# A filler sweep that projects the merge gates before the branch gates

## The chip, the core and the metric

The kernel runs on one core of a Trainium2 chip. Its engines work from queues of their own, each in a fixed order: TensorE (PE), VectorE (DVE), ScalarE (ACT), GpSimd (POOL), and SyncE (SP), which here only issues DMAs. ACT and POOL issue DMAs too. The metric is the time of one execution on the device in microseconds, lower is better.

## What is computed

One step of a decoder layer for 2048 prompt tokens and 32 sample tokens (8 groups of 4), in fp32:

```python
h = _rmsnorm(x, g_pre) @ w_in
qa, ka, va, za, ub, zb, qc, zc, gt = jnp.split(h, SPLITS, axis=-1)
# A: dilated window attention -> oa; B: conv, LayerNorm, swish -> ob; C: attention into a memory -> oc
gates = jax.nn.sigmoid(gt).reshape(Bx, S, 3, D_MODEL)
mix = (gates[..., 0, :] * ((oa * jax.nn.silu(za)) @ w_pa)
       + gates[..., 1, :] * ((ob * jax.nn.silu(zb)) @ w_pb)
       + gates[..., 2, :] * ((oc * jax.nn.silu(zc)) @ w_pc))
y = x + _rmsnorm(mix @ w_out, g_post)
```

The case concerns the columns of `w_in` for za (768), zb (768), zc (512) and the merge gates gt (3072). They are not needed until the last phase.

## The kernel before

Activations are kept transposed, with 128 channels on the partitions and tokens along the free axis. Every fp32 operand is split into a high and a low part, and a product is three matmuls (lines 166, 167, 168 in `gemm`: high by high, high by low, low by high). A block is 128 output columns of `w_in`. Its weights are one DMA of 512 KB (line 150), split on POOL (lines 55 and 56).

Phase A1 normalizes the tokens and computes q, k, v, the convolution input and qc, with the convolution's taps on DVE (line 322). The LayerNorm of the convolution then runs in steps of 256 tokens (`conv_norm`, lines 663 to 686): a load, a sum on DVE (665), a matmul with ones on PE (667), a subtraction (668), squares on ACT (671), a sum (673), a matmul (675), variance and reciprocal root on DVE and ACT (677, 63 to 68), scaling (679), per-channel scale on POOL (681), tanh on ACT (684), and a product on DVE (685). Beside it the memory's keys and values are projected (917 to 947), and the prompt's and sample's attention into the memory follow. After it come the sample attention (791 to 869) and the prompt attention, six head pairs with two heads each (571 to 652). At the end of a pair the three dilation patterns are combined: statistics go through DRAM (427 to 441), coefficients come back as broadcast DMAs `cb<-d_cf` (448), and DVE and POOL multiply and add (451 to 453). Phase C multiplies branch outputs by their gates z (1139), splits them (1197 on ACT, 1198 on DVE), projects and merges (1150 to 1155), and applies the output projection (1178 to 1180).

The sweep is a generator that runs beside all of this from the LayerNorm to the end of the attention. It computes the 40 blocks of za, zb, zc and gt. The tokens come in three thirds of 768, 768 and 544, of whose normalized values one is held at a time; at the start of the second and third POOL loads the next one (1083). In each third the sweep takes the blocks in the order of a list, and each block in chunks of 256 tokens (288 at the very end): 3, 3 and 2 chunks, so 120, 120 and 80, 320 in all. A chunk is 24 matmuls into one of two PSUM buffers `gg`, followed by the part of `chunk` that reads it into one of two staging tiles `st`:

```python
elif kind == "gt":
    nc.scalar.activation(st[:, :n], p[:, :n], AF.Tanh, scale=0.5)                      # line 243, ACT
else:
    nc.scalar.activation(st[:, :n], p[:, :n], AF.Tanh, scale=0.5)                      # line 245, ACT
    nc.vector.scalar_tensor_tensor(st[:, :n], st[:, :n], 1.0, p[:, :n],
                                   op0=ALU.add, op1=ALU.mult)                          # line 246, DVE
if dst is not None:
    q.dma_start(dst[j][:, s:s + n], st[:, :n])                                         # line 248, ACT's queue
```

So a gate chunk (gt) is finished by ACT, while a z chunk (za, zb, zc) needs ACT and then DVE, reads PSUM in both, and its store on ACT's queue waits for DVE. 192 chunks are of the first kind and 128 of the second.

No loop in the program interleaves the sweep with the rest. Its instructions are written last (one call, `self.fill(1000)`), and the builder orders each engine's instructions by a timeline that it estimates, in which what is written earlier goes first and the sweep fills what is left. The order is fixed when the program is built. The first block's weights are loaded ahead, at the end of phase A1 (`self.early`).

Of the kernel before, what the change touches and what calls it, by code (L numbers as in the profile page):

```python
# [26 lines left out]
EARLY = 1  # L27
# [7 lines left out]
CQ, CK, CV, CZA, CUB, CZB, CQC, CZC, CGT = 0, 768, 1536, 2304, 3072, 4608, 5376, 5888, 6400  # L35


class K:
# [134 lines left out]
    def phase_a1(self, wp, blocks=None):  # L173
        tc, nc, I, O = self.tc, self.nc, self.I, self.O
        with tc.tile_pool(name="x12", side="right", bufs=1) as xpool, \
                tc.tile_pool(name="stg", side="right", bufs=3) as stg, \
                tc.tile_pool(name="sm1", side="right", bufs=2) as small, \
                tc.tile_pool(name="wr", side="right", bufs=2) as self.wr, \
                tc.tile_pool(name="psg", side="right", bufs=4, space=PSUM, reuse_waits="tile") as psg, \
                tc.tile_pool(name="pst", side="right", bufs=3, space=PSUM, reuse_waits="tile") as pst:  # L180
            for th in (1, 2):
                n = THIRDS[th][1]
                self.X[th] = tuple([xpool.tile([128, n], R32, name=f"x{th}{c}{k}") for k in range(8)]
                                   for c in "hl")
            with tc.tile_pool(name="xst", side="right", bufs=7) as xst:
                st = self.stage_x(xst, small, pst)
                next(st)
                self.consts(self.cpool, xst, pst)
                ws = [self.load_w(wp, self.win(CQ), 8, rp=self.wr)]
                for _ in st:  # L190
                    pass
            with tc.tile_pool(name="brw", side="right", bufs=1) as bp:
                self.taps(self.cpool, bp, pst)
                self.bias_rows(self.cpool, bp, pst)

            out = [(th, c, k) for th in (1, 2) for c in range(2) for k in range(8)]

            with tc.tile_pool(name="cnv", side="right", bufs=1, reuse_waits="tile") as cnv:
                ws.append(self.load_w(wp, self.win(CQ + 128), 8, rp=self.wr))
                for cs, js in [(c, j) for c in (CHUNKS[:1], CHUNKS[1:2], CHUNKS[2:3], CHUNKS[3:4], CHUNKS[4:]) for j in range(2)]:  # L200
                    for s, n in cs:
                        self.chunk("q", js, s, n, ws[js], stg, psg, "g", pst)
                order = []
                rest = [("k", j) for j in range(6)] + [("v", j) for j in range(6)] + \
                       [("q", j) for j in range(2, 6)] + [("qc", j) for j in range(4)]
                for j in range(6):
                    order += [("u", j)] + rest[:3]
                    rest = rest[3:]
                order += rest
                for kind, j in order:  # L210
                    if blocks is not None and (kind, j) not in blocks:
                        continue
                    if kind == "u":
                        gs = self.blk_u(j, wp, stg, cnv, psg, pst)
                        with self.later(LAG):
                            self.conv(j, cnv, pst, *gs)
                    else:
                        self.blk_x(kind, j, wp, stg, psg, pst)
                    for th, c, k in out[:2]:
                        nc.sync.dma_start(self.d_x[th][c][k], self.X[th][c][k].bitcast(F32))  # L220
                    del out[:2]
                assert not out
                self.early = {("za", j): self.load_w(wp, self.win(CZA + 128 * j), 8, rp=self.wr) for j in range(EARLY)}
    def blk_x(self, kind, j, wp, stg, psg, pst):
        w = self.load_w(wp, self.win(self.BASE[kind] + j * 128), 8, rp=self.wr)
        for s, n in CHUNKS:
            self.chunk(kind, j, s, n, w, stg, psg, "g", pst)
# [973 lines left out]
    def build(self):  # L1201
        tc, nc = self.tc, self.nc
        with tc.tile_pool(name="dr", bufs=1, space=DRAM) as dp, tc.tile_pool(name="cst", bufs=1) as cp:
            self.scratch(dp)
            self.cpool = cp
            with tc.tile_pool(name="x0", bufs=1) as x0, tc.tile_pool(name="w1", bufs=2) as wp:
                self.X = [tuple([x0.tile([128, 768], R32, name=f"x0{c}{k}") for k in range(8)] for c in "hl"), None, None]
                self.phase_a1(wp)
                with tc.tile_pool(name="gst", bufs=2, reuse_waits="tile") as gp, tc.tile_pool(name="pgg", bufs=2, space=PSUM, reuse_waits="tile") as pgg:
                    blocks = [(k, j) for k, n in (("za", 6), ("zb", 6), ("zc", 4), ("gt", 24)) for j in range(n)]  # L1210
                    self.filler, self.credit = self.sweep(blocks, x0, wp, gp, pgg), 0
                    with tc.tile_pool(name="sbk", side="right", bufs=1, reuse_waits="tile") as sk:
                        self.memory()
                        self.sample_bias(sk)
                        self.sample_attention()
                    self.attention(list(range(HA)))
                    self.fill(1000)
            self.phase_c()
# [89 lines left out]
```

## Time and profile before

| | us |
|---|---|
| median of 3 runs (3150.18 to 3156.21) | 3155.59 |
| the profiled execution, its own time | 3154.4 |
| its span from first to last instruction | 3152.6 |
| PE busy | 3000.2 |
| DVE busy | 2014.8 |
| ACT busy | 1124.2 |
| POOL busy | 1350.4 |
| first and last matmul of the sweep | 868.7 and 2549.7 |

Times in the views count from the first instruction. "Busy" of PE is the time in which any matmul is under way; idle time of an engine is put down to what ended it, written with an arrow (`PE gg L166 <- DVE st L246`: a matmul into `gg`, line 166, waited for line 246 on DVE). Names are the program's tiles with their numbers left out, written out<-in. A wait is one inferred from semaphores; where an instruction waits for several, the last one is named. The granted clock is the share of full speed that TensorE was given.

### The profile page before, as it was taken

What the parts mean: (1) busy time and instruction counts of PE and PEld (TensorE: products, weight loads), DVE (VectorE), ACT (ScalarE), POOL (GpSimd) and SP (SyncE); (2) the same over time, 40 slices, a digit from 0 to 9 for tenths busy, and PEclk for the clock granted to TensorE, in tenths of its full rate; (3) what the DMA queues carried; (4) which work ended last, traced back from release to release, by engine and by line L of the source; (5) the groups of instructions that cost most, each with busy time, mean ns of one, the idle gap of its engine ahead of it and who ended that gap; (6) DMA issues with size and microseconds to landing.
All of it is one profiled execution on the core that took longest, in us unless ns stands there. A gap on an engine that the chain in (4) does not pass through costs nothing.

```text
span 3152.6 us, 55374 instructions
## 1 busy us (share of the span) xinstructions
PE 3000.2 (95%) x20705; PEld 2839.9 (90%) x20705; DVE 2014.8 (64%) x3734; ACT 1124.2 (36%) x2835; POOL 1350.4 (43%) x1048
## 2 busy tenths in 40 slices
PE   7999999999987999999999999989899979999998
PEld 6899999999987999998999999989898967787897
DVE  5297797796677926465546766666656457556563
ACT  5010010010132433243437575656565523222221
POOL 0121221142356537444256565667676433233240
PEclk9899999999999999999999999999999989999999
DMA  7232222211265454477454656576555487657561
GB/s 250 85 103 80 80 60 61 63 62 50 81 182 167 135 153 144 147 219 239 151 139 116 161 123 163 128 185 150 156 143 152 109 279 227 223 168 227 161 197 53
DMA packets 532218, 454.66 MB, mean 144 GB/s; under 512 B 118191, under 2 KB 458581, under 8 KB 531137
## 3 DMA queue, kind: packets, MB, share of 16 engines
q1 hardware_dynamic: 357502, 335.36, 36.2%
q10 hardware_dynamic: 169840, 105.02, 11.7%
q0 software_dynamic: 4608, 10.75, 1.2%
q8 instruction: 164, 2.69, 0.4%
q14 instruction: 104, 0.85, 0.1%
HBM read 332.96 MB, written 118.04 MB: 143 GB/s over the span
## 4 chain that ended last, share of the span: by engine, by line
PE 70%; DMA 12%; DVE 7%; issue 4%; POOL 3%; ACT 2%; SPq 1%; ACTq 0%; DVEq 0%; POOLq 0%
PE g L166 8%; PE g L167 8%; PE g L168 8%; PE gg L166 6%; PE gg L168 6%; PE gg L167 6%; PE pg L168 3%; PE pg L166 3%; PE pg L167 3%; PE pt L571 2%; DMA cb<-d_cf 2%; PE y L1180 2%; PE y L1179 2%; PE y L1178 2%; PE o L598 1%
## 5 line engine op out<-in xcount | busy, mean ns | idle before, releaser
L166 PE MATMUL gg<-x0h,whi 128*128 128x256 f32 (+1 forms) x2560 | 747.9, 292 | 25.9 <-DVE st L246 12.2
L168 PE MATMUL gg<-x0h,wlo 128*128 128x256 f32 (+1 forms) x2560 | 741.8, 290 | 0.1
L167 PE MATMUL gg<-x0l,whi 128*128 128x256 f32 (+1 forms) x2560 | 741.1, 290 | 0.0
L55 POOL TENSOR_SCALAR whi<-wraw 128x1024 fp32r<-128x1024 f32 x162 | 242.7, 1500 | 928.5 <-PE g L167 524.1
L166 PEld LDWEIGHTS gg<-x0h,whi 128*128 128x128 f32 x2560 | 493.2, 193 | 35.0 <-DVE st L246 13.7
L167 PEld LDWEIGHTS gg<-x0l,whi 128*128 128x128 f32 x2560 | 493.5, 193 | 2.2 <-issue 0.5
L168 PEld LDWEIGHTS gg<-x0h,wlo 128*128 128x128 f32 x2560 | 493.2, 193 | 2.2 <-POOL wlo L56 0.3
L322 DVE SCALAR_TENSOR_TENSOR acc<-G,cw,acc 128x1536 f32<-128x1536 f32 (+15 forms) x354 | 480.8, 1408 | 0.3
L56 POOL TENSOR_TENSOR wlo<-wraw,whi 128x1024 fp32r<-128x1024 f32 x162 | 417.0, 2575 | 9.4 <-PE gg L168 0.2
L155 POOL TENSOR_TENSOR clo<-craw,chi 128x768 fp32r<-128x768 f32 (+1 forms) x96 | 174.1, 1815 | 346.0 <-ACT chi L154 329.8
L627 ACT ACTIVATE P<-T,stm 128x128 f32<-128x128 f32 (+1 forms) x576 | 260.8, 455 | 141.0 <-DVE stm L625 94.8
L239 ACT ACTIVATE st<-g 128x384 f32<-128x384 f32 (+1 forms) x132 | 60.2, 461 | 570.7 <-PE g L168 550.7
L166 PE MATMUL pg<-ac,chi 128*128 128x512 f32 (+1 forms) x640 | 229.4, 359 | 16.6 <-ACT chi L154 8.7
L625 DVE CUSTOM_DVE_ANT_0 T<-s,bias 128x128 f32<-128x128 f32 (+1 forms) x576 | 191.5, 357 | 80.8 <-PE s L617 47.0
L167 PE MATMUL pg<-ac,chi 128*128 128x512 f32 (+1 forms) x640 | 228.8, 358 | 6.3 <-DVE ac L1198 6.3
L168 PE MATMUL pg<-ac,clo 128*128 128x512 f32 (+1 forms) x640 | 227.6, 357 | 3.6 <-POOL clo L155 3.6
L576 DVE TENSOR_TENSOR pl<-pt,ph 128x512 fp32r<-128x512 f32 x240 | 155.6, 652 | 52.4 <-ACT ph L575 48.9
L168 PE MATMUL g<-x0h,wlo 128*128 128x384 f32 x544 | 184.3, 339 | 2.9 <-POOL wlo L56 2.9
L166 PE MATMUL g<-x0h,whi 128*128 128x384 f32 x544 | 183.6, 338 | 2.6 <-ACT st L239 2.3
L167 PE MATMUL g<-x1l,whi 128*128 128x384 f32 x544 | 186.0, 342 | 0.0
L167 PE MATMUL g<-x0l,whi 128*128 128x384 f32 x544 | 185.8, 342 | 0.0
L168 PE MATMUL g<-x1h,wlo 128*128 128x384 f32 x544 | 185.8, 342 | 0.0
(330 smaller groups left out, 7425.0 us busy)
## 6 DMA issues: line engine op xcount, KB each, us to landing
wraw<-in_w_in ACTq DMA_DIRECT2D x119, 512.0 KB
d_g<-st ACTq DMA_DIRECT2D x168, 128.0 KB
cb<-d_cf SPq DMA_DIRECT2D x72, 256.0 KB
g<-d_g SPq DMA_DIRECT2D x72, 256.0 KB
wraw<-in_w_in SPq DMA_DIRECT2D x35, 512.0 KB
kvc<-in_cache_k_win SPq DMA_DIRECT2D x8, 1536.0 KB
kvc<-in_cache_v_win SPq DMA_DIRECT2D x8, 1536.0 KB
raw<-d_q SPq DMA_DIRECT2D x48, 256.0 KB
```

The costliest lines, as they stand in the source:

```text
L55: nc.gpsimd.tensor_scalar(hi, raw, 1.0, 1.0, op0=ALU.mult, op1=ALU.mult)
L56: nc.gpsimd.tensor_sub(lo, raw, hi.bitcast(F32))
L155: nc.gpsimd.tensor_sub(lo, raw, hi.bitcast(F32))
L166: nc.tensor.matmul(ps, hi[:, k, :], h, start=k == 0, stop=False)
L167: nc.tensor.matmul(ps, hi[:, k, :], l, start=False, stop=False)
L168: nc.tensor.matmul(ps, lo[:, k, :], h, start=False, stop=k == kb - 1)
L322: nc.vector.scalar_tensor_tensor(a3[:, lo:hi], G[:, src:src + hi - lo, 2 - m:130 - m], w, a3[:, lo:hi], op0=ALU.mult, op1=ALU.add)
L571: nc.tensor.transpose(t[:, 128 * x:128 * x + 128], pc, self.ident)
L576: nc.vector.tensor_tensor(pl[:, :w], t[:, :w], ph[:, :w].bitcast(F32), op=ALU.subtract)
L625: nc.vector.tensor_tensor_reduce(sc[:, :w], t[:, o:o + w], bias[:, 256 - w:256], 1.0, 3.0e38, ALU.add, ALU.min, m)
L627: nc.scalar.activation(P[:, o:o + w], sc[:, :w], AF.Exp, bias=m, scale=-1.0, accum_out=self.stl[:, col:col + 1])
L1178: nc.tensor.matmul(y[:m, c, :], ah[:, ts_], bh[:, cs], start=k == 0, stop=False)
```

## The change

The list of blocks puts the 24 gate blocks ahead of the 16 z blocks, in each third of the tokens; and the block whose weights are loaded ahead is the first gate block instead of the first block of za.

```diff
-                self.early = {("za", j): self.load_w(wp, self.win(CZA + 128 * j), 8, rp=self.wr) for j in range(EARLY)}
+                self.early = {("gt", j): self.load_w(wp, self.win(CGT + 128 * j), 8, rp=self.wr) for j in range(EARLY)}
...
-                    blocks = [(k, j) for k, n in (("za", 6), ("zb", 6), ("zc", 4), ("gt", 24)) for j in range(n)]
+                    blocks = [(k, j) for k, n in (("gt", 24), ("za", 6), ("zb", 6), ("zc", 4)) for j in range(n)]
```

The instructions are the same in number and kind. Three places show how their order moved; in all, `st` and `gg` belong to the sweep.

On ACT, where the sweep begins (the LayerNorm's first squares are L671, the memory's L915, the square root L63), before:

```order
L245 ACTIVATE st<-gg 128x256 x2
L150 DMA wraw<-in_w_in 128x8x128 x2
L915 ACTIVATE msq,mss<-mt 128x1024
L671 ACTIVATE sq<-c 128x1536
L248 DMA d_za_76<-st 128x256 x2
L915 ACTIVATE msq,mss<-mt 128x1024
L63 ACT_TABLE_LOAD
```

and with the change:

```order
L243 ACTIVATE st<-gg 128x256 x2
L150 DMA wraw<-in_w_in 128x8x128
L248 DMA d_g_124<-st 128x256
L915 ACTIVATE msq,mss<-mt 128x1024
L671 ACTIVATE sq<-c 128x1536
L248 DMA d_g_124<-st 128x256
L150 DMA wraw<-in_w_in 128x8x128
L915 ACTIVATE msq,mss<-mt 128x1024
L243 ACTIVATE st<-gg 128x256
L248 DMA d_g_124<-st 128x256
```

Gate chunks stand where chunks of za stood, their stores a little earlier.

On DVE, one step of the LayerNorm (from the sum of squares L673 to the product L685; `mrow` is the memory's), before:

```order
L673 TENSOR_REDUCE sm<-sq 128x256
L665 TENSOR_REDUCE sm<-c 128x256
L246 SCALAR_TENSOR_TENSOR st<-st,gg 128x256
L945 COPY mrow<-tr 128x256
L677 TENSOR_SCALAR var<-sco 128x256
L945 COPY mrow<-tr 128x256
L246 SCALAR_TENSOR_TENSOR st<-st,gg 128x256
L668 SCALAR_TENSOR_TENSOR c<-str,c 128x1536
L64 RECIPROCAL lnr<-lns 128x256
L246 SCALAR_TENSOR_TENSOR st<-st,gg 128x256
L65 TENSOR_TENSOR lns<-lnr 128x256
```

and with the change:

```order
L673 TENSOR_REDUCE sm<-sq 128x256
L665 TENSOR_REDUCE sm<-c 128x256
L677 TENSOR_SCALAR var<-sco 128x256
L64 RECIPROCAL lnr<-lns 128x256
L668 SCALAR_TENSOR_TENSOR c<-str,c 128x1536
L65 TENSOR_TENSOR lns<-lnr 128x256
L66 TENSOR_TENSOR lns<-lns,var 128x256
L67 TENSOR_SCALAR lns<-lns 128x256
L68 TENSOR_TENSOR lnr<-lns,lnr 128x256
L679 TENSOR_TENSOR c<-c,lnr 128x1536
```

The sweep has left DVE's queue in this stretch.

On DVE, the last head pair's combination, after the last attention matmul (L440 the coefficients, L451 to L453 the sum of the patterns, L1198 the first splits of phase C), before:

```order
L440 TENSOR_TENSOR ew<-ew,wsum 32x384
L451 TENSOR_TENSOR O<-O,cb 128x1024 x2
L452 TENSOR_TENSOR O<-O 128x1024
L451 TENSOR_TENSOR O<-O,cb 128x1024
L453 TENSOR_TENSOR O<-O 128x1024
L451 TENSOR_TENSOR O<-O,cb 128x1024
L452 TENSOR_TENSOR O<-O 128x1024
L1198 TENSOR_TENSOR ac<-araw,ac 128x512 x2
```

and with the change:

```order
L451 TENSOR_TENSOR O<-O,cb 128x1024
L246 SCALAR_TENSOR_TENSOR st<-st,gg 128x288
L451 TENSOR_TENSOR O<-O,cb 128x1024
L452 TENSOR_TENSOR O<-O 128x1024
L246 SCALAR_TENSOR_TENSOR st<-st,gg 128x256
L451 TENSOR_TENSOR O<-O,cb 128x1024
L246 SCALAR_TENSOR_TENSOR st<-st,gg 128x288
L453 TENSOR_TENSOR O<-O 128x1024
L246 SCALAR_TENSOR_TENSOR st<-st,gg 128x256
L451 TENSOR_TENSOR O<-O,cb 128x1024
L452 TENSOR_TENSOR O<-O 128x1024
L246 SCALAR_TENSOR_TENSOR st<-st,gg 128x288
```

Here the sweep has entered DVE's queue: the last five chunks, all z, are finished between instructions that wait for DMA.

## The prediction

> **What bounds the kernel now.** I read the page first, then the busy time of each engine by stage (columns: stretch, its length, busy time and instructions of PE, weight loads, DVE, ACT and POOL, granted clock, DMA share, GB/s).
>
> ```profile
> span 3152.6 us, 55374 instructions
> PE 3000.2 (95%) x20705; PEld 2839.9 (90%) x20705; DVE 2014.8 (64%) x3734; ACT 1124.2 (36%) x2835; POOL 1350.4 (43%) x1048
> ...
> 868.00:1130.00 262.00, 225.24 (x1743) 217.45 (x1742) 207.94 (x275) 97.50 (x180) 150.55 (x135) 0.95 0.53 163
> 1130.00:1310.00 180.00, 180.00 (x1441) 173.87 (x1440) 71.95 (x171) 60.28 (x167) 91.93 (x80) 1.00 0.43 132
> 1310.00:1670.00 360.00, 347.42 (x2670) 327.63 (x2668) 198.88 (x445) 149.25 (x354) 167.93 (x211) 0.99 0.62 185
> 1670.00:2100.00 430.00, 413.32 (x3422) 408.37 (x3420) 282.50 (x833) 274.73 (x843) 261.94 (x217) 0.98 0.58 144
> 2100.00:2510.00 410.00, 389.94 (x3125) 385.08 (x3126) 262.56 (x781) 250.73 (x767) 274.87 (x220) 0.98 0.58 145
> 2510.00:2553.00 43.00, 38.94 (x298) 37.54 (x297) 12.75 (x16) 8.41 (x19) 23.85 (x14) 0.99 0.77 222
> 2553.00:2600.00 47.00, 32.47 (x114) 24.17 (x114) 30.33 (x38) 16.52 (x22) 13.41 (x9) 0.82 0.93 308
> ```
>
> PE is the bound: 3000.2 of 3152.6 us. Its work does not change, so only its idle time can. That idle time, row by row, is 36.8 us in 868 to 1130 (convolution's LayerNorm, memory keys and the first z blocks), nothing in 1130 to 1310, 12.6 in the sample attention, 16.7 and 20.1 in the two halves of the prompt attention, 4.1 in the tail where only the sweep is left, 14.5 at the start of phase C. The first of these holds most, and DVE is busy 207.94 of 262 us there. A time saved there stays saved: the next stretch has PE busy all through, with gate blocks. The waits of PE in 860 to 1140 (total, times, longest):
>
> ```profile
> PE sco L675 <- DVE sm L673: 14.9, 5, 9.0
> PE gg L166 <- DVE st L246: 10.1, 9, 1.8
> PE str L667 <- DVE sm L665: 4.5, 5, 1.4
> ...
> PE gg L166 <- POOL whi L55: 3.9, 1, 3.9
> ```
>
> So two things hold PE there. A sweep chunk waits for its PSUM buffer until L246 has read it, 10.1 us; and a LayerNorm matmul stands in PE's queue before DVE has its sums ready, 14.9 + 4.5 = 19.4 us. Both end on DVE.
>
> **The change, term by term.** All counts stay: 320 chunks, 128 of them with L246. What moves is where those 128 stand.
>
> *Term 1, the LayerNorm stretch.* The groups of DVE in 868 to 1110 (busy, mean ns, idle before):
>
> ```profile
> L685 DVE SCALAR_TENSOR_TENSOR c<-sq,c 128x1536 f32<-128x1536 f32 x7 | 32.5, 4648 | 14.0 <-ACT sq L684 14.0
> ...
> L246 DVE SCALAR_TENSOR_TENSOR st<-st,gg 128x256 f32<-128x256 f32 x46 | 18.5, 408 | 3.8 <-ACT st L245 3.8
> ...
> L679 DVE TENSOR_TENSOR c<-c,lnr 128x1536 f32<-128x1536 f32 x7 | 12.3, 1752 | 0.1
> ```
>
> All L246 go from here, 18.5 us of DVE. Gate chunks are read by ACT alone, whose tanh (0.38 to 0.41 us in the rows of the tail below) both kinds need. The 10.1 us of waits for L246 cannot occur; part comes back, since ACT is in order too and its LayerNorm squares wait for DVE. The second gain is in the LayerNorm chain. One step of it, DVE and then ACT, by time:
>
> ```profile
> 952.66 2.79 DVE L673 TENSOR_REDUCE sm<-sq 128x256 f32<-128x1536 f32 x1 [1.55 <-ACT sq L671]
> 955.37 2.79 DVE L665 TENSOR_REDUCE sm<-c 128x256 f32<-128x1536 f32 x1
> 958.08 0.41 DVE L246 SCALAR_TENSOR_TENSOR st<-st,gg 128x256 f32<-128x256 f32 x1
> ...
> 958.74 0.41 DVE L677 TENSOR_SCALAR var<-sco 128x256 f32<-128x256 f32 x1
> ...
> 963.92 0.42 DVE L246 SCALAR_TENSOR_TENSOR st<-st,gg 128x256 f32<-128x256 f32 x1 [0.79 <-ACT st L245]
> 964.26 0.42 DVE L65 TENSOR_TENSOR lns<-lnr 128x256 f32<-128x256 f32 x1
> 958.52 0.33 ACTq L248 DMA_DIRECT2D d_za<-st  x1
> 960.64 0.42 ACT L63 ACTIVATE lns<-var 128x256 f32<-128x256 f32 x1
> ```
>
> L677 stands behind an L246 (0.3 to 0.4 us); L65 behind one that itself had waited 0.79 us for ACT (1.1 us together). ACT's queue held the store of a z chunk until 958.52, because that store waits for L246, and only then came to the square root L63. So a step of this chain loses roughly 1 to 2 us to z chunks, and the stretch holds eight such steps of 256 columns: 8 to 16 us of chain. What PE gets of it is bounded. Below: if the chain alone sets the pace and only the 0.4 us before L677 goes in each of 8 steps, 3 us. Above: all waits on DVE, 10.1 + 19.4, about 29 us. The two gains overlap, since a PE that no longer waits for L246 comes earlier to the LayerNorm matmul and waits there. I take 12 us, a little over the waits on L246, because the chain that then receives PE is itself shorter by about as much. **Term 1: -12 us** (-29 to -3).
>
> [...]
>
> *Term 2, where the 128 go in the sample and prompt attention.* In the first third 48 of them move to about 1310 to 1440, while those of the second third leave 1460 to 1685; both are sample attention or its border. The second third's 48 move to the prompt attention around 1970 to 2100, and the last third's 32 from 2120 to 2298 to the end. L246 in 1440 to 1690, and then in 2100 to 2310, with who waited for it:
>
> ```profile
> L246 DVE SCALAR_TENSOR_TENSOR st<-st,gg x48: 400/420/424, 1460.4 to 1685.4; 128x256 f32<-128x256 f32 x48
> ...
>   PE gg L166: 1.6, 2
> ```
> ```profile
> L246 DVE SCALAR_TENSOR_TENSOR st<-st,gg x32: 403/430/456, 2119.5 to 2298.9; 128x256 f32<-128x256 f32 x16, 128x288 f32<-128x288 f32 x16
> ...
>   PE gg L166: 0.6, 1
> ```
>
> At these prices the sample attention comes out even (1.6 in, 1.6 out), and the prompt attention gains one or two waits, 0.6 us each. One thing is dearer: at the border between two head pairs DVE stands still for the coefficients' DMA (L451), and PE with it:
>
> ```profile
> 2245.48 0.55 PE L597 MATMUL o<-ph,V 128*128 128x256 f32 x1 [4.97 <-DVE O L644]
> 2385.31 0.45 PE L597 MATMUL o<-ph,V 128*128 128x128 f32 x1 [3.21 <-DVE O L644]
> ```
>
> The first border has z chunks in the sweep, the second gate chunks: 1.8 us apart. Before, one border carried z chunks; now two do, besides the tail. **Term 2: +2 us** (-2 to +6: none, or 1.8 us on each border and 1 us of waits per third).
>
> *Term 3, the tail.* After the last attention matmul only sweep chunks are left, now z chunks, and DVE holds their L246 between the four L451 that wait for DMA. Before:
>
> ```profile
> 2541.34 1.68 DVE L451 TENSOR_TENSOR O<-O,cb 128x1024 f32<-128x1024 f32 x1 [13.57 <-DMA cb<-d_cf]
> ...
> 2550.72 1.29 DVE L451 TENSOR_TENSOR O<-O,cb 128x1024 f32<-128x1024 f32 x1 [4.63 <-DMA cb<-d_cf]
> ...
> 2556.00 1.22 DVE L451 TENSOR_TENSOR O<-O,cb 128x1024 f32<-128x1024 f32 x1 [2.87 <-DMA cb<-d_cf]
> 2557.26 1.23 DVE L452 TENSOR_TENSOR O<-O 128x1024 f32<-128x1024 f32 x1
> 2538.01 0.41 ACT L243 ACTIVATE st<-gg 128x288 f32<-128x288 f32 x1 [1.58 <-PE gg L168]
> 2540.86 0.38 ACT L243 ACTIVATE st<-gg 128x256 f32<-128x256 f32 x1 [2.44 <-PE gg L168]
> 2551.12 1.15 ACT L1197 ACTIVATE ac<-araw 128x512 fp32r<-128x512 f32 x2 [0.66 <-POOL O L451]
> 2551.81 1.04 PE L166 MATMUL pg<-ac,chi 128*128 128x512 f32 x3 [1.79 <-ACT ac L1197]
> 2559.15 0.80 PE L167 MATMUL pg<-ac,chi 128*128 128x512 f32 x1 [6.30 <-DVE ac L1198]
> ```
>
> The fifth chunk from the end was read at 2538.4. Now its L246 stands behind the first L451, which ends at 2543.0, so its buffer is free at 2543.5. The chunk after next would have begun at 2540.9 and stalls 2.6 us. The last chunk stalls in the same way behind the third L451 (2552.0), about 2.9 us, and ends near 2555.6. Most of this is hidden: phase C's matmuls really began at 2559.15, held by the attention's last sum. What is not hidden is the last L246. It stands behind the fourth L451 and L452 (2558.5), ACT issues its store behind it (0.33 us), and only then do the 0.6 us of L1197 and the 0.7 us of L1198 follow, so phase C starts near 2560.7, not 2559.1. **Term 3: +2 us** (0, if the DMA is early enough, to +8, if both stalls of PE and the late start add up).
>
> Sum: 3154.4 - 12 + 2 + 2 = 3146.4 us in the terms of the profiled execution, which is 1.2 us below the median of 3155.59. So 3147 us, to the nearest.
>
> **Rivals.** *The LayerNorm chain sets the pace* (chance 0.24). The 9.0 us wait at L675 speaks for it: behind one slow L685 no order of the sweep helps. Then the waits for L246 only change their name to L673, term 1 is 3 us, and the rest takes 4 back: 3155. Against it: the chain itself carries about six L246 in each step (46 in eight).
>
> *The late evictions cost more than they spare* (0.16). Place: the tail and the two borders. If the coefficients' DMA is later than the builder assumed, as it was by up to 13.57 us, each L246 behind an L451 also holds ACT, whose next instruction is a store waiting for it, and so the exponentials. With term 3 at 8, term 2 at 6 and term 1 at 3 the sum is +11: 3166. It decides from the point where terms 2 and 3 pass term 1. Against it: 0.6 us for 32 chunks in 2100 to 2310.
>
> *The stretched L685 go too* (0.10). (4648 - 1752) x 7 = 20.3 us of the chain is L685 above the time of L679. If the new order keeps POOL's work away from it, term 1 reaches its end: 3154.4 - 29 + 4, about 3130 with the median's offset. [...]
>
> That the change does nothing is small: the order of every engine shows gates first.
>
> **How the numbers follow.** Forecast 0.50, rivals 0.24, 0.16, 0.10. About 0.2%, 6.3 us, is what a measurement of this kernel can tell from no change: faster is below 3149.3, slower above 3161.9. The forecast alone covers 3138 to 3152 (term 1 from -19 to -7), of which I put 0.42 below 3149.3 and 0.08 above. Faster: 0.42 + 0.10 = 0.52. Slower: 0.16 of the second rival. Same: 0.32. The range for 8 in 10 is 3135 to 3162: it leaves out most of the third rival and the worse part of the second.
>
> **What would show it.** The LayerNorm's matmuls L675 before:
>
> ```profile
> L675 PE MATMUL sco<-sm,ones x18: 190/380/796, 886.3 to 1127.4; 128*128 128x256 f32 x16, 128*128 128x32 f32 x2
> ```
>
> In the stretch from 868 us, L246 is gone from the waits of PE, the last L675 comes about 12 us before its old 1127.4, and the waits for L673 do not grow past 19.4 us. Between 1130 and 1310 PE stays full. Near the end, L246 stands behind L451 and phase C's matmuls start 2 us later relative to the attention's end. I am wrong if L673 takes up what L246 gave (first rival), if PE's idle time in the prompt attention grows past 45 us (second), or if L685 falls to 1.8 us (third).

## The result: slower by 0.6%

The changed kernel takes 3171.88 us (median; 3154.0 to 3185.82), the kernel before, run beside it, 3151.24 us (3145.0 to 3161.4). The ratio is 1.0057, with a 95% interval of 1.0036 to 1.0078: about 18 us lost, where 8 us less had been forecast. The changed kernel's runs also lie further apart, over 32 us instead of 16.

### The profile page after: what moved, and what is told of

It reads as the page before. It is cut to its first block, busy times and chain, and to the rows that moved or that the text cites. A ratio compares the mean times of both kernels' runs of the same rounds, so it can differ in the third digit from the quotient of the medians.

```text
span 3170.3 us, 55440 instructions
## 1 busy us (share of the span) xinstructions
PE 3014.4 (95%) x20705; PEld 2851.0 (90%) x20705; DVE 2020.4 (64%) x3734; ACT 1122.8 (35%) x2835; POOL 1354.8 (43%) x1048
## 3 DMA queue, kind: packets, MB, share of 16 engines
q1 hardware_dynamic: 357502, 335.36, 35.9%
## 4 chain that ended last, share of the span: by engine, by line
PE 72%; DMA 12%; DVE 7%; issue 3%; POOL 3%; ACT 2%; SPq 1%; ACTq 0%; DVEq 0%; POOLq 0%
PE g L166 8%; PE g L167 8%; PE g L168 8%; PE gg L166 6%; PE gg L167 6%; PE gg L168 6%; PE pg L168 3%; PE pg L166 3%; PE pg L167 3%; PE pt L571 3%; DMA cb<-d_cf 2%; PE s L616 2%; PE o L598 2%; PE s L617 2%; PE y L1178 2%
## 5 line engine op out<-in xcount | busy, mean ns | idle before, releaser
L166 PE MATMUL gg<-x0h,whi 128*128 128x256 f32 (+1 forms) x2560 | 749.9, 293 | 30.8 <-DMA x0h<-d_x 12.3
L55 POOL TENSOR_SCALAR whi<-wraw 128x1024 fp32r<-128x1024 f32 x162 | 243.8, 1506 | 939.8 <-PE g L167 525.2
L56 POOL TENSOR_TENSOR wlo<-wraw,whi 128x1024 fp32r<-128x1024 f32 x162 | 422.0, 2606 | 14.4 <-PE gg L168 2.8
L576 DVE TENSOR_TENSOR pl<-pt,ph 128x512 fp32r<-128x512 f32 x240 | 155.5, 652 | 48.3 <-ACT ph L575 44.1
```

What stands on the lines that cost most here:

```text
L55: nc.gpsimd.tensor_scalar(hi, raw, 1.0, 1.0, op0=ALU.mult, op1=ALU.mult)
L56: nc.gpsimd.tensor_sub(lo, raw, hi.bitcast(F32))
L166: nc.tensor.matmul(ps, hi[:, k, :], h, start=k == 0, stop=False)
L576: nc.vector.tensor_tensor(pl[:, :w], t[:, :w], ph[:, :w].bitcast(F32), op=ALU.subtract)
```

## The profile after

First the head of the page, of the changed kernel and then of the kernel before and the changed one profiled a second time (span; busy time of the engines):

```profile
span 3170.3 us, 55440 instructions
PE 3014.4 (95%) x20705; PEld 2851.0 (90%) x20705; DVE 2020.4 (64%) x3734; ACT 1122.8 (35%) x2835; POOL 1354.8 (43%) x1048
```
```profile
span 3148.1 us, 55374 instructions
PE 2993.6 (95%) x20705; PEld 2834.1 (90%) x20705; DVE 2016.9 (64%) x3734; ACT 1125.3 (36%) x2835; POOL 1353.9 (43%) x1048
```
```profile
span 3164.5 us, 55440 instructions
PE 3014.7 (95%) x20705; PEld 2853.1 (90%) x20705; DVE 2018.7 (64%) x3734; ACT 1122.3 (35%) x2835; POOL 1352.4 (43%) x1048
```

These lines hold the result. Span less busy PE is PE's idle time: 152.4 (3152.6 - 3000.2, the prediction's lines) and 154.5 us before, 155.9 and 149.8 after. On average it has not changed. What grew is PE's busy time, from 3000.2 and 2993.6 to 3014.4 and 3014.7 us: 17.6 us more for the same 20705 matmuls, and the spans differ by 17.1. The same matmuls took longer. The stages of the changed kernel, in the columns of the prediction's table:

```profile
868.00:1130.00 262.00, 235.61 (x1838) 228.71 (x1838) 200.24 (x228) 99.88 (x186) 156.85 (x142) 0.96 0.55 168
1130.00:1310.00 180.00, 180.00 (x1450) 174.46 (x1449) 82.18 (x203) 58.36 (x165) 92.87 (x79) 1.00 0.43 133
1310.00:1670.00 360.00, 342.63 (x2570) 320.71 (x2570) 178.07 (x426) 151.47 (x361) 169.71 (x208) 0.97 0.63 186
1670.00:2100.00 430.00, 409.11 (x3390) 405.88 (x3388) 287.17 (x849) 262.78 (x811) 255.07 (x212) 0.98 0.55 137
2100.00:2510.00 410.00, 386.38 (x3057) 381.35 (x3058) 267.34 (x777) 252.72 (x774) 274.14 (x218) 0.96 0.56 145
```

In the LayerNorm stretch PE is busy for 235.61 us instead of 225.24 and finishes 1838 matmuls instead of 1743. In the sample attention it finishes 2570 instead of 2670, and the clock column falls to 0.97; from 2100 it falls to 0.96.

To add clock to idle time, I read the granted clock in windows of 2 us and sum up 1 minus the clock, times 2 us: "lost clock". Idle time plus lost clock, in us, from two traces of each kernel (phase C begins 16 to 22 us later after the change, so the tail and phase C go together):

| stage | before | after | change of the means |
|---|---|---|---|
| up to 868 | 29.0+11.9, 29.5+6.8 | 28.5+13.7, 27.7+13.7 | +3.2 |
| LayerNorm, 868 to 1130 | 36.8+13.6, 37.3+13.6 | 26.4+10.2, 25.8+12.0 | -13.4 |
| 1130 to 1310 | 0 | 0 | 0 |
| sample attention, 1310 to 1670 | 12.6+3.4, 10.6+1.7 | 17.4+10.3, 16.4+12.0 | +13.9 |
| prompt attention, 1670 to 2510 | 36.7+18.8, 43.0+22.2 | 44.5+27.3, 40.8+27.3 | +9.6 |
| tail and phase C | 37.3+18.4, 34.1+11.9 | 39.2+13.4, 39.0+17.0 | +3.4 |

The gain in the LayerNorm stretch is there, in both traces, and as large as forecast. The sample attention alone takes it back, and the prompt attention and small pieces make the loss. The first row is a measure of chance: PE's order is the same in both kernels up to 889 us, and still the executions differ there by up to 6 us. In sum the loss is lost clock, 78.3 us on average after and 61.2 before, because the idle time that the LayerNorm stretch gave up came back behind it.

Some of the lost clock falls into idle time and counts twice in this table. Counted only while PE is busy, it is 52.4 and 44.1 us before, 65.8 and 68.1 after. Busy time less this lost clock is 2947.8, 2949.6, 2948.6 and 2946.7 us, the same in all four traces, so the clock is the whole of the busy time's growth. By stage the changes are then +3.1, -12.0, 0, +13.0, +8.0 and +6.0.

How a wait becomes lost clock can be seen at one place of the prompt attention of the changed kernel: PE's rows in order of time, then windows of 2 us (the clock is third from the end).

```profile
1795.31 0.28 PE L168 MATMUL gg<-x0h,wlo 128*128 128x256 f32 x1
1799.32 0.48 PE L616 MATMUL s<-KH,QS 128*128 128x128 f32 x1 [3.72 <-POOL QS L491]
1799.59 0.42 PE L617 MATMUL s<-KL,QS 128*128 128x128 f32 x1
...
1800.34 0.41 PE L166 MATMUL gg<-x0h,whi 128*128 128x256 f32 x1
```
```profile
1796.00:1798.00 2.00, 0.00 (x0) 0.00 (x0) 2.00 (x7) 1.25 (x5) 2.00 (x1) 1.00 0.57 175
1798.00:1800.00 2.00, 0.68 (x3) 0.68 (x4) 1.36 (x6) 0.22 (x1) 2.00 (x4) 0.66 0.37 142
1800.00:1802.00 2.00, 2.00 (x12) 2.00 (x11) 0.30 (x2) 0.16 (x1) 2.00 (x4) 0.50 0.90 248
1802.00:1804.00 2.00, 2.00 (x12) 2.00 (x11) 0.43 (x2) 1.69 (x5) 2.00 (x3) 0.50 0.41 140
1804.00:1806.00 2.00, 2.00 (x13) 2.00 (x12) 1.34 (x4) 1.84 (x6) 1.92 (x2) 0.64 0.00 0
```

PE stands for 3.72 us and then runs at a clock of 0.50 for about 7 us: the sweep's matmul takes 0.41 us here and 0.28 before the wait. PE counts as busy while it runs at the half clock (2.00 of 2.00 us in the third and the fourth of these windows). The wait of 3.72 us costs 3.4 us more than its own length.

## Experiments

All times are medians in us, each beside the kernel before on the same chip. The kernels that give each third its own order have `for kind, j in blocks[th]:` in the sweep; "old" is the order before, `z` its 16 z blocks and `g` its 24 gate blocks.

| run | time | before | ratio (95%) |
|---|---|---|---|
| e1_first | 3153.36 | 3151.52 | 1.0002 (0.9989 to 1.0016) |
| e2_second | 3164.06 | 3151.52 | 1.0038 (1.0026 to 1.0051) |
| e3_third | 3158.75 | 3151.52 | 1.0023 (1.0011 to 1.0034) |
| e4_noz | 3135.98 | 3151.52 | 0.9951 (0.9936 to 0.9965) |
| e5_sp | 3207.88 | 3152.71 | 1.0172 (1.0159 to 1.0185) |
| e7_mid | 3152.43 | 3152.71 | 1.0000 (0.999 to 1.001) |
| e9_between | 3161.39 | 3152.71 | 1.0022 (1.0005 to 1.0039) |
| e8_defer | 3146.39 | 3152.71 | 0.9976 (0.9964 to 0.9988) |
| e10_old_nowait | 3136.99 | 3152.72 | 0.9958 (0.994 to 0.9975) |
| e11_new_nowait | 3139.0 | 3152.72 | 0.9959 (0.9948 to 0.9971) |
| e12_one | 3154.36 | 3152.72 | 1.0010 (0.9996 to 1.0024) |
| e13_new_noz23 | 3170.44 | 3152.72 | 1.0057 (1.0039 to 1.0075) |
| e14_mid_nowait | 3123.12 | 3146.49 | 0.9924 (0.9898 to 0.9949) |
| e15_first_nowait | 3144.78 | 3146.49 | 0.9994 (0.9979 to 1.0009) |
| e16_noz_nowait | 3118.73 | 3146.49 | 0.9907 (0.9884 to 0.993) |

Where I compare runs of different chips below, I go by the ratio, times 3152.

**One third at a time.** Theory A, at first, was the second rival: a late z block has a price by its place. Theory B: any new order moves where PE meets the waits of the prompt attention.

```diff
-blocks = [(k, j) for k, n in (("za", 6), ("zb", 6), ("zc", 4), ("gt", 24)) for j in range(n)]
+blocks = [g + z, old, old]     # e1_first
+blocks = [old, g + z, old]     # e2_second
+blocks = [old, old, g + z]     # e3_third
```

> Only the first third takes gates first; thirds two and three stand as in the kernel before (3151). Theory A (each z block has a price by its place: dear in the LayerNorm stretch, and in the changed kernel dear at the borders of the prompt attention): the 14 us of the LayerNorm stretch stay gained (10 us of idle time, 3 us of clock), the sample attention takes 5 to 12 back, the prompt attention is as before; 3140 to 3149. Theory B (every new order of the sweep moves where PE meets the waits of the prompt attention, by a scheduler's chance, and the changed kernel drew a bad one): the gain in the LayerNorm stretch stands, but the prompt attention may lose as much as in the changed kernel; 3150 to 3165.

> Only the second third takes gates first, so that its z blocks stand from about 1970 to 2100 us, at two head-pair borders. Theory A: the prompt attention loses what the changed kernel lost there, about 16 us of idle time and clock, less 1 to 3 us in the sample attention, where its z blocks left; 3162 to 3168. Theory B: no tie to the z blocks; the waits at the borders differ from the kernel before, but not more where z blocks stand; 3145 to 3165.

> Only the last third takes gates first, so that its z blocks end the sweep. Theory A: phase C starts about 2 us later and one border of the prompt attention is 2 us cheaper; 3149 to 3155, within what can be told from the kernel before. Theory B: 3145 to 3165.

Measured by the ratios: +1, +12 and +7 us. The three add up to +20, about the whole change (+18). The first third alone, where the forecast's gain is, comes out even: its trace shows 35.9 us of idle time and lost clock in the LayerNorm stretch (50.4 before), but 42.9 in the sample attention (16.0 before), and 47.2 in the prompt attention (55.5 and 65.2 before).

The second third's loss does not stand where its z blocks stand. The trace of e2_second has 57.6 us in the prompt attention, no more than before, and 61.6 behind 2510 us (55.7 and 46.0 before). PE waits 12.1 us there for the first merge of phase C (L1150), which stands in VectorE's queue behind the last pair's L451; before, its waits for L1150 at this place were 3.4 and 1.8 us. The last third costs 7, not the 2 of the tail; its trace is of the fastest of its runs (3152.76) and does not show where.

**The eviction itself.**

```diff
             nc.scalar.activation(st[:, :n], p[:, :n], AF.Tanh, scale=0.5)
-            nc.vector.scalar_tensor_tensor(st[:, :n], st[:, :n], 1.0, p[:, :n], op0=ALU.add, op1=ALU.mult)   # e4_noz, old order
+            if s < 768: nc.vector.scalar_tensor_tensor(...)                                                  # e13_new_noz23, changed order
```

> The order of the kernel before, but the z chunks leave out their second eviction step on VectorE (st = (st + 1) * psum), so that a z chunk is evicted as a gate chunk is, and the place of the z blocks can no longer matter; za, zb and zc are then wrong, the rest is computed. Theory A: what the z blocks cost anywhere goes: the 14 us of the LayerNorm stretch and a few us later; 3130 to 3140. Theory B: the LayerNorm stretch gains its 14 us, the rest draws anew; 3135 to 3165.

> The changed order, with L246 left out of the z chunks of the second and last third (80 of 128; they are evicted as gates, so za, zb and zc are wrong there). Theory A (the z chunks' eviction is what costs there): the 20 us of those thirds go; 3145 to 3155, as in the run with gates first in the first third only, or below. Theory B: the place of the waits is drawn anew, with or without L246; 3145 to 3170.

Without any L246 the kernel takes 15 us less than before: this is what the 128 products on VectorE cost in the old order. But taking 80 of them out of the second and last third of the changed order gave nothing in the total: +18, as with them. Theory A, which gave these thirds' evictions some 20 us, falls as a price of each z block. Its trace shows more than the total: the prompt attention is back at 58.7 us, as before the change, and the loss stands in the sample attention (27.2), where the first third keeps its L246, and behind 2510 us (61.5, beside 55.7 and 46.0 before). PE's order, too, is drawn anew from 1841 us on, so the edit does not change the evictions alone.

**ScalarE held by the stores.**

```diff
-            q.dma_start(dst[j][:, s:s + n], st[:, :n])
+            (nc.sync if kind in ("za", "zb", "zc") else q).dma_start(dst[j][:, s:s + n], st[:, :n])
```

> The changed order, with the store of each z chunk issued by SyncE instead of ScalarE, so that ScalarE no longer stands until VectorE has done L246. If the late z blocks are dear because ScalarE is held (theory A1: its exponentials and evictions come late), most of the 20 us comes back: 3150 to 3158. If they are dear through VectorE's own time, or through the PSUM buffer that L246 frees late (A2), it stays at 3165 to 3175. SyncE, which issues the loads of the attention, may be held instead; then it is slower than 3175.

54 us slower than before: SyncE, which also issues the attention's loads, then stands 220.8 us in 73 waits for L246. The edit moved the wait to a worse queue, so it does not tell whether ScalarE's was the harm. In e13_new_noz23 the stores of the later thirds wait for no L246, and the total did not fall.

**Other places for the z blocks.**

```diff
+blocks = [g[:17] + z + g[17:], old, old]                                                     # e7_mid
+blocks = [old, g[:14] + z[:6] + g[14:18] + z[6:11] + g[18:22] + z[11:] + g[22:], old]        # e9_between
+blocks = [old, g[:1] + z + g[1:], old]                                                       # e12_one
```

> Only the first third differs from the kernel before: 17 gate blocks, then the 16 z blocks (51 to 99 of its 120 chunks, about 1115 to 1330 us, where TensorE has no idle time), then 7 gate blocks. If the gates-first order loses in the sample attention what it gains in the LayerNorm stretch (theory A, as the run with only the first third suggests), this keeps the gain of 14 and loses little: 3137 to 3143. If every new order draws anew (theory B): 3145 to 3165.

> Only the second third differs from the kernel before: its z blocks are spread over the prompt attention (chunks 162 to 179, 192 to 206, 219 to 233) but not over the stretches behind the end of a head pair (182 to 187, 208 to 213, 234 to 239), which carry gates. If z blocks are dear at these borders only: 3150 to 3156, where gates first in this third gave 3164. If they are dear anywhere in the prompt attention: 3160 to 3166.

> The kernel before with one gate block moved ahead of the z blocks in the second third alone: three chunks shift by 48, everything that a theory of z blocks counts stays (no z block comes to a border of the prompt attention). Theory A: 3150 to 3154. Theory B (every new order draws its waits at the borders anew): it differs from the kernel before by up to 10 us either way, with a wider spread of its runs.

In the middle of the first third the z blocks leave the LayerNorm stretch (35.6 us of idle time and lost clock) and hardly touch the sample attention (21.3 instead of 16.0). Still the total is that of the kernel before: the prompt attention, whose own blocks stand in the old order, went from 55.5 and 65.2 to 67.0 in its one trace. Keeping z away from the borders of the second third left +7 beside +12, with intervals that overlap; its trace, like that of e2_second, has no more in the prompt attention than before (58.5) and more behind 2510 us (60.3). Moving one gate block changed nothing that can be told, although PE's order is another from 1484 us on: a new order alone need not cost anything.

**The waits at the borders.** What the prompt attention has at each border, whatever the sweep does, is L451, which waits for coefficients that go through DMAs. Here it reads rows that were written long before, and so leaves the real coefficients out:

```diff
-                    src = self.d_cf[hp][g:g + 1, a * S + half * 1024:a * S + half * 1024 + 1024]
+                    src = self.d_q[hp][g + 3 * a:g + 3 * a + 1, half * 1024:half * 1024 + 1024]
```

> The order of the kernel before; the combination of a head pair reads its coefficients cb from rows of d_q, written long before, instead of from d_cf, which is computed from this pair's statistics. So L451 no longer waits for that chain of DMAs (the prompt attention's result is wrong by it, its instructions are the same). Theory B (the time behind each head pair is set by how far the coefficients' DMA comes later than VectorE's fixed order assumes): the 8 to 15 us of idle time and clock at each of five borders shrink; 3125 to 3140. Theory A (the price is that of the z chunks' own evictions): 3145 to 3152.

> The same edit on the changed order. Theory B: with the waits for coefficients gone the changed order keeps its gain in the LayerNorm stretch and lies 8 to 14 us below the run of the old order with this edit. Theory A: it stays 10 to 20 us above it.

This removes the whole difference of the two orders: -13 us for the old one, -31 for the changed one (from +18 to -13). Both stand at the same time. The waits of VectorE and GpSimd at L451 fall from 42.6 and 69.5 us to 1.2 and 8.6 in the old order, from 45.4 and 85.1 to 1.9 and 15.1 in the changed one (1670 to 2600). The builder also draws the order anew: PE's differs from 1627 us on in the old order, from 1609 in the changed one. So the edit removes the waits together with the order that was built around them. The prompt attention of the two (old, then changed):

```profile
1670.00:2510.00 840.00, 812.03 (x6690) 805.36 (x6689) 576.22 (x1631) 532.92 (x1625) 572.09 (x442) 0.98 0.58 148
```
```profile
1670.00:2510.00 840.00, 809.53 (x6649) 801.73 (x6648) 590.28 (x1657) 523.68 (x1609) 558.55 (x437) 0.98 0.58 148
```

Idle time is 28.0 and 30.5 us, lost clock 13.7 and 13.6, where the changed kernel had 44.5 and 27.3. Theory B is right that the time at the borders hangs on the waits for coefficients. It was wrong in its second half: the changed order does not come out 8 to 14 us ahead. The sample attention takes 35.2 us in it, 25.4 in the old order with the same edit.

**Where the LayerNorm gain goes.** With the waits at the borders away, the first third is seen alone:

> The coefficients cb from rows of d_q as before (no wait at the borders; the prompt attention's result is wrong), with the z blocks of the first third in its middle (17 gate blocks, 16 z, 7 gates). If the 13 us that the LayerNorm stretch gains are real and are given back in the sample attention, then this order, whose z blocks lie mostly in the full stretch from 1130 to 1310, keeps them less about 5: 3127 to 3132, against 3137 for the old order with this edit. If the gain is given back wherever the z blocks go: 3135 to 3140.

> The same edit, with gates first in the first third only. If the sample attention gives back what the LayerNorm stretch gains, and the rest of the loss was the borders' waits: 3136 to 3141, as the old order (3137) and the changed one (3139) with this edit. If gates first in the later thirds has its own price of some us even without the waits: below the changed order's 3139 by as much.

> The same edit, and L246 left out of every z chunk (za, zb, zc wrong too). It gives the whole price of the 128 L246 with the borders' waits away: if that is the 10 to 13 us of the LayerNorm stretch and a few more: 3121 to 3127. If without L246 the total stays at 3133 or more, the 15 us that leaving it out gave beside the waits were won at the borders.

With the z blocks of the first third in its middle the total falls by 24 us, 11 more than the old order with this edit (the intervals just touch): here the gain of the LayerNorm stretch is in the total at last. With gates first in the first third only it falls by 2, 11 less than the old order: in that order the z blocks of the first third and of the second follow each other, 96 chunks through the whole sample attention. LayerNorm stretch and sample attention, z in the middle and then gates first in the first third:

```profile
868.00:1130.00 262.00, 238.19 (x1861) 231.37 (x1861) 196.93 (x233) 100.51 (x188) 154.88 (x142) 0.96 0.56 171
...
1310.00:1670.00 360.00, 344.34 (x2610) 324.33 (x2609) 195.08 (x453) 158.96 (x379) 164.67 (x210) 0.98 0.64 190
```
```profile
868.00:1130.00 262.00, 236.14 (x1843) 229.21 (x1842) 202.45 (x228) 100.08 (x187) 155.05 (x142) 0.97 0.55 169
...
1310.00:1670.00 360.00, 334.20 (x2437) 311.16 (x2437) 192.72 (x457) 147.94 (x352) 161.54 (x204) 0.94 0.63 183
```

The first stretch is the same in both. In the second, PE does 2610 matmuls in the one and 2437 in the other, at clocks of 0.98 and 0.94. Without L246 and without the waits the total falls by 29 us, 16 more than with L246, so the 15 us of e4_noz were the price of L246 and not won at the borders. In all three runs the order behind is drawn anew as well.

**A version that is faster than both.** The z chunk is evicted by a copy, and its tanh and product are made in phase C:

```diff
-            nc.scalar.activation(st[:, :n], p[:, :n], AF.Tanh, scale=0.5)
-            nc.vector.scalar_tensor_tensor(st[:, :n], st[:, :n], 1.0, p[:, :n], op0=ALU.add, op1=ALU.mult)
+            nc.scalar.activation(st[:, :n], p[:, :n], AF.Copy)
...
+                        nc.scalar.activation(z[:, :n], z[:, :n], AF.Tanh, scale=0.5)
+                        nc.vector.scalar_tensor_tensor(raw[:, :n], z[:, :n], 1.0, raw[:, :n], op0=ALU.add, op1=ALU.mult)
```

> The order of the kernel before, but ScalarE evicts a z chunk by a plain copy, and its tanh and product are made in phase C, on 64 tiles of 512 or 544 columns (one more instruction of ScalarE and one of VectorE each). The sweep is then rid of L246 as in the run without it (3136). Phase C gains 64 x about 1.2 us on VectorE, 28% idle there, partly ahead of its first matmuls: 3138 to 3150. If VectorE's time in phase C is on the path: 3150 to 3190.

It takes 0.9976 of the time before (0.9964 to 0.9988), 8 us less, about half of what leaving L246 out gave. Its trace has 57 us of idle time and lost clock in tail and phase C, where the run without L246 has 49. Since z and gate chunks are evicted alike in it, the order of the sweep should matter less; that was not run.

**Which losses repeat.**

> The kernel before, profiled a second time, to see how far its stages repeat. Both theories: idle time and lost clock of the LayerNorm stretch (868 to 1130) and the sample attention (1310 to 1670) within 4 us of 50 and 16; those of the prompt attention (1670 to 2510) may move by 10 us, since its borders wait for DMAs.

> The changed kernel, profiled a second time. If the stages of its first trace are the order's own and not that execution's: LayerNorm stretch 37 (13 below the kernel before), sample attention 26 to 28 (11 above), prompt attention 62 or more, where the first trace had 72 and the kernel before 55.

Their times are 3149.88 and 3166.28. The LayerNorm stretch (50.9, 37.8) and the sample attention (12.3, 28.4) repeat within 4 us, the prompt attention (65.2, 68.1) does not: it moved by 10 us in the kernel before. The means of both traces stand in the table above.

## Why the prediction was wrong

**The first step, "its work does not change, so only its idle time can", failed.** Idle time did not change in sum, as the four heads of the page show; busy time grew by 17.6 us with the same matmuls, all of it lost clock. I had the clock column before me (0.95 to 1.00 up to 2553 us) and priced each wait at its own length. It is not the only failure: by idle time alone the change comes to nothing instead of 8 us won, and that is term 2's.

**Term 1 (-12) was right in place and size.** The waits of PE from 860 to 1140 in the changed kernel (total, times, longest), and the LayerNorm matmuls:

```profile
PE sco L675 <- DVE sm L673: 8.1, 5, 3.7
PE gg L166 <- POOL whi L55: 5.8, 1, 5.8
PE kv L971 <- ACT sP L1004: 5.6, 4, 3.1
PE str L667 <- DVE sm L665: 2.9, 5, 1.2
```
```profile
L675 PE MATMUL sco<-sm,ones x18: 276/379/796, 889.4 to 1119.9; 128*128 128x256 f32 x16, 128*128 128x32 f32 x2
```

L246 is gone from the list, L673 and L665 together went from 19.4 to 11.0 us, and the idle time of the stretch fell by 10.9 us, with 2.5 us of clock beside it. The waits for L246, L673 and L665 lost 18.5 us in all; others took part of it back (POOL whi L55 from 3.9 to 5.8, ACT sP L1004 from 1.1 to 5.6). I had not worked this out, so that the size fits so well is in part luck. The last L675 came 7.5 us sooner, not 12. The first rival, that L673 takes up what L246 gave, did not occur. Between 1130 and 1310 PE is full, as said.

**Term 2 (+2) failed, in both its parts; it measured +24 by the table, +21 with the clock counted only while PE is busy.** "The sample attention comes out even" held for what I priced, the waits for L246: 0.9 us of the changed kernel beside 1.3 before in these lists of 1310 to 1670, before and then after:

```profile
PE gg L166 <- DMA x0h<-d_x: 5.3, 4, 2.0
PE S L804 <- ACT KTh L794: 3.2, 2, 2.8
PE gg L166 <- DVE st L246: 1.3, 1, 1.3
PE tr L862 <- DVE vl L856: 0.8, 1, 0.8
```
```profile
PE gg L166 <- DMA x0h<-d_x: 7.3, 4, 2.8
PE tr L862 <- DVE vl L856: 3.1, 2, 2.1
PE S L805 <- ACT KTh L794: 1.7, 1, 1.7
...
PE gg L166 <- DVE st L246: 0.9, 2, 0.8
```

What came in is other waits, for the split of the values (vl) and the reload of x0, each short, and 8.6 us of lost clock. I priced an eviction by the waits that carry its name; it can also move the order in which ScalarE and VectorE serve the attention. That the first third's z blocks do it is shown by moving them: in the middle of that third the sample attention had 21.3 and 24.2 us, behind all gates 27.6 and 28.4, and next to the second third's z blocks 42.9 and 46.3. By which instruction it passes is not shown.

At the borders the price was not 1.8 us for z chunks. The second rival named the place, the coefficients' late DMA, and its 3166 was near the time. That is luck: it had term 1 at -3 and its loss at L246 behind L451 holding ScalarE, and without L246 in these thirds the total did not come back. The waits of PE in 1670 to 2510, before and then after:

```profile
PE s L616 <- DVE stm L625: 10.3, 6, 3.2
PE o L597 <- DVE O L644: 8.6, 3, 5.0
...
PE s L616 <- POOL QS L491: 2.0, 2, 1.0
```
```profile
PE s L616 <- POOL QS L491: 11.8, 3, 5.1
PE o L597 <- DVE O L644: 9.1, 5, 4.2
PE o L598 <- DVE pl L576: 6.8, 5, 2.5
...
PE gg L166 <- DMA x0h<-d_x: 5.1, 1, 5.1
```

The largest is one that I had not named: the queries QS, made by GpSimd (11.8 us; 6.4 in the second trace, 2.0 in both before). At the third border they stand in GpSimd's queue behind an L451 that waits for coefficients. GpSimd there, before and then after:

```profile
2099.48 2.36 POOL L451 TENSOR_TENSOR O<-O,cb 128x1024 f32<-128x1024 f32 x1 [4.11 <-DMA cb<-d_cf]
...
2104.48 2.40 POOL L491 TENSOR_SCALAR QS<-QS 128x512 fp32r<-128x512 f32 x4
```
```profile
2088.36 3.95 POOL L451 TENSOR_TENSOR O<-O,cb 128x1024 f32<-128x1024 f32 x1 [10.00 <-DMA cb<-d_cf]
...
2119.24 2.34 POOL L451 TENSOR_TENSOR O<-O,cb 128x1024 f32<-128x1024 f32 x1 [9.14 <-DMA cb<-d_cf]
2121.55 3.33 POOL L491 TENSOR_SCALAR QS<-QS 128x512 fp32r<-128x512 f32 x4
```

In the changed kernel the queries come 17 us later there, of which its border itself begins 9 us later (the statistics of the head pair are copied by L516 at 2051.92, before at 2043.24). PE waits 5.1 us for them, and some 20 us sooner it had waited 5.1 us for x0. The last coefficients are requested by SyncE when cb's two buffers come free, before and then after:

```profile
2087.88 0.45 SPq L448 DMA_DIRECT2D cb<-d_cf  x1
...
2089.43 0.45 SPq L448 DMA_DIRECT2D cb<-d_cf  x1
```
```profile
2101.57 2.37 SPq L448 DMA_DIRECT2D cb<-d_cf  x2
```

They are 12 to 14 us later. In each kernel the queues' order is fixed when it is built, but not how late the coefficients are: in the two traces of the kernel before, GpSimd waited 69.5 and 63.1 us for them. Over all borders it is GpSimd's waits at L451 that grew (1670 to 2600, before and then after), while VectorE's stayed (42.6 and 45.4 us):

```profile
POOL O L451 <- DMA cb<-d_cf: 69.5, 11, 9.0
```
```profile
POOL O L451 <- DMA cb<-d_cf: 85.1, 12, 10.0
```

The second traces repeat it, with 63.1 and 85.4. In e13_new_noz23 they are 64.4, as before the change. What stays open is why they grow in the changed kernel, by the evictions themselves or by the order that was drawn around them, and why the time then shows up behind 2510 us where they do not grow. My own mark for this, more than 45 us of idle time in the prompt attention, was not passed (44.5 and 40.8), because the loss went into the clock (20.5 on average before, 27.3 after).

**Term 3 (+2) is not told apart from chance** (+3.4 for tail and phase C, +6.0 with the clock counted only while PE is busy, and executions that differ by more). The stalls of the tail came as worked out, one after the other:

```profile
2538.37 0.36 PE L166 MATMUL gg<-x0h,whi 128*128 128x256 f32 x1 [1.19 <-DVE st L246]
...
2546.33 0.36 PE L166 MATMUL gg<-x0h,whi 128*128 128x256 f32 x1 [1.48 <-DVE st L246]
...
2557.59 0.40 PE L166 MATMUL gg<-x0h,whi 128*128 128x288 f32 x1 [2.12 <-DVE st L246]
...
2566.96 0.61 PE L166 MATMUL gg<-x0h,whi 128*128 128x288 f32 x1 [3.08 <-DVE st L246]
```

They sum to 7.9 us; I had 2.6 and 2.9. From the last matmul of the attention to the first of phase C, idle time and the clock lost in busy time went from 3.9 and 1.8 us to 11.4 and 11.1; behind it they went from 45.2 and 39.7 to 38.9 and 41.1. So less of it was hidden than I had worked out. In e3_third, which changes this third alone and lost 7 us, the tail is not told apart from its two borders.

**The third rival** (L685 falls to 1.8 us) did not occur, or only in part: L685 averages 3470 ns from 868 to 1120 us in the changed kernel, 4648 before. The trace before shows what goes with a long L685: the three longest took 12.6, 7.8 and 3.6 us with 11.0, 6.2 and 1.9 us of GpSimd's splits (L55, L56) beside them, which leaves 1.6 us each time; the one with none beside it, at 1009.39 us, took 1.8. Why they go together was not shown. The change has fewer such meetings (19.9 us of splits beside its eight L685, 24.6 before), and nothing in its list of blocks was aimed at them.

The chances were wrong above all in giving 0.16 to "slower": the two stages of 360 and 840 us behind the stretch, full of waits of one to five us, had been taken as nearly fixed. Two slips of arithmetic changed little: the sum is 3147.6, so 3148 to the nearest, and term 1 at -19 gives 3141, not 3138.

## What to carry to other kernels

Read busy time at equal counts, not idle time alone. Here 19 waits of 3 us or more on the engine that bounds the kernel averaged 3.9 us, with 3.1 us of lost clock each, so an estimate for such a wait in this kernel is nearly twice its length. A gain in one stage of a statically ordered program is only safe if the stages behind it keep their order; where they hold waits for DMAs that the order cannot foresee, first see what those waits cost, as by leaving the DMA's real source out, and expect that an edit may move them. And before work is moved off a loaded engine, look whether it can be left to a stage with room: deferring the product won 8 us.

## What the runs showed of the hardware

The granted clock fell to 0.50 behind waits of PE, short ones among them. In the two traces of each kernel, from 1130 to 2510 us, it dropped 44 times. The lost clock of a drop was 1.7, 3.4 or 5.1 us, so the half clock lasted 3.4, 6.8 or 10.2 us. Counting each drop for the longest wait beside it (within 3.4 us, as long as the shortest drops), 19 of 20 waits of PE of 3 us or more had one, 15 of 24 of 2 to 3 us, 9 of 30 of 1 to 2 us, and 1 of 62 of 0.3 to 1 us.

The spread of a kernel's runs goes in part with the clock. Of the changed kernel's runs, the one of 3156.61 us had a mean clock of 0.980, the one of 3185.82 us one of 0.974; 0.006 of 3170 us is 19 of the 29 us between them. The clock is not all of it: a run of 3171.56 us had 0.974 as well.
